# Placement of the down-weight block operations in the first feed-forward block and of the seven-product down projection in the third, in a hybrid decoder layer

## The chip, the core and the metric

The program runs on one core of one Trainium2 chip. The metric is the device time of one execution in microseconds (us). The engines are TensorE (PE, with its weight loads shown as PEld), VectorE (DVE), ScalarE (ACT), GpSimd (POOL) and the DMA queue that SyncE issues (SP). Each engine runs its own instructions in order and waits at an instruction until the semaphores it needs are there.

## The reference

One layer of a decoder is computed in float32 for a prompt of 2048 positions and 32 sample positions: RMSNorm, an input projection, dilated attention beside a spatial gating unit, an output projection with residual, and then the part that this case is about:

```
def _swiglu(x, g, w_gate, w_up, w_down):
    h = _rmsnorm(x, g)
    return (jax.nn.silu(h @ w_gate) * (h @ w_up)) @ w_down
...
    x = x + _swiglu(x, norm2_g, w_gate, w_up, w_down)
```

The model width is 1024 and the hidden width 2816, which is 22 column tiles of 128. A final RMSNorm follows.

## The kernel before

**Precision.** Every matrix product is made of three products of a high and a low part (high with high, high with low, low with high). The high part is a rounded copy made by ACT, the low part is the difference, made by POOL or DVE (`both_halves`: ACT at L1604, then POOL at L1608).

**Blocks and units.** The 16 prompt tiles are worked in three blocks: tiles 0 to 5, 6 to 11, and 12 to 15. The third block also takes the sample rows along. Inside a block the loop runs over f, the 22 column tiles of the hidden width, and for each f over q from 0 to 6: one seven-product (Strassen-like) scheme makes gate and up together from seven products instead of eight. `product` (L1714 to L1716) is one such gate or up product: four steps k of three matmuls, into one of four PSUM banks named ps_m. Behind each product DVE or ACT combine its result (L1726 on ACT for q=0; on DVE L1728, L1730, L1740, L1743 with L1744, L1746 and L1752 for q=1 to 6). An even f and the odd f behind it form a pair; the hidden values of a pair go through the down projection together, while the next even f is worked.

**First block: plain down projection.** `down_unit` projects one tile: two halves of six matmuls each (L1975), each half into one of two PSUM banks named ps_o, and then DVE adds the half to the accumulator (L1977). A half can only start when the add of the half two before it has freed its bank. For even f the loop puts two tiles behind q=3, two behind q=4 and two behind q=5.

**First block: preparing the down weights of the later blocks.** The second and third block use a seven-product scheme for the down projection too, and its operands are made once, in the first block, from the raw weight rows of a pair in the buffers `fe` (rows2[1]) and `fd` (rows2[0]): four differences `block_sum` (DVE, L1653), then for each a rounded high part `block_high` (ACT, L1661), a low part `block_low` (DVE, L1666) and its store to memory `block_keep` (SP, L1670). The table `FIRST_DOWNS` says behind which (f mod 2, q) each is issued, and with a third number, behind which point of the down tiles. `first_downs_ahead` reads it.

**Other first-block work in those queues.** ACT scales fresh weights (L1576, in groups of eight), POOL forms their sums (L1588, L1591, L1594, L1597) and low halves (L1608), and ACT rounds those sums (L1604, `op<-pair` or `op<-fr`).

**Second and third block: seven products.** Class `Seven` queues the down projection of a pair as single products (`one`, L1917, three matmuls of 512 columns, and a DVE add at L1919) and, in the third block, sample products (`sample`, L1925 and L1928). In the third block that is 14 products and 4 sample products for each pair. `begin` fills the queue when the even f reaches a given q, and `woven` returns a step function that `product` calls behind each of its four k: it pops one entry. All entries alternate between two PSUM banks, so each waits for the add of the entry two before it. `even`, `odd_a`, `odd_b` and `odd_c` make the seven left operands from the hidden values (high part on ACT L1834, low part on DVE L1835, sums on DVE L1859, L1869, L1875, L1882), and `plan` says behind which q `even` runs and behind which q the right operands `whole[d]` are loaded (SP, L1830).

**Order.** There is no planner here: within each engine the instructions stand in the order in which the loops write them. `later(n, ...)` puts work off by n `tick`s, one per product or down tile.

Of the kernel before, what the change touches and what calls it, by code (L numbers as in the profile page):

```python
# [28 lines left out]
NF = FF // P  # L29
# [36 lines left out]
def hymba_step(ctx: ExitStack, tc: tile.TileContext, A: dict, O: dict):  # L66
# [6 lines left out]
    left, low, right = ExitStack(), ExitStack(), ExitStack()  # L73
# [585 lines left out]
    for n in range(len(first) + 4):  # L659
        if n >= 4:  # L660
            (w_split if first[n - 4][0] == "w" else x_half_split)(*first[n - 4][1:])
        if n < len(first):
            if first[n][0] == "w":
                k = first[n][1]
# [39 lines left out]
    for half in range(2):  # L704
        for ki, kind in enumerate(ORDER[half]):
            for gi, tiles in enumerate(GROUPS):
                start = ((half * 5 + ki) * 3 + gi) * 8
                for k in range(KD):
                    if start == 0:

                        for j in range(3):
                            n = 3 * k + j
# [7 lines left out]
                for j, tj in enumerate(tiles):  # L720
# [23 lines left out]
                    else:  # L744
                        layer_norm(e + 1, t, lambda t=t: zn["g", t], P)

                        f = e + 4 + (3 if tj in (4, 5) else 0)
                        at(f, "turn", gate_split, t)
                        if tj % 4 == 3:
                            g = t // 4  # L750
# [448 lines left out]
    for h in range(H):  # L1199
# [4 lines left out]
        if end:  # L1204

            x = s0 - NI
            d = stats_of(h, dve, steps_of(x, (11, "misc"), (13, "early"), (14, "early")))
# [8 lines left out]
        if ahead:  # L1216
            d = stats_of(h, pool, steps_of(s0, (2, "misc"), (4, "early"), (5, "early")))
            weights_of(d, steps_of(s0, (5, "misc"), (6, "early"), (6, "misc"), (7, "early"), (7, "misc"), (9, "early"), (9, "mid")))
            chunks = ((11, 14), (11, 16), (14, 19), (18, 22))
        else:  # L1220
            d = stats_of(h, pool, steps_of(s0, (3, "misc"), (5, "early"), (6, "early")))
# [11 lines left out]
    for i, it in enumerate(items):  # L1233
        x, h, n = B0 + i, it["h"], it["n"]
# [443 lines left out]
    def split_down(f):  # L1678
# [1 line left out]
        split_sb(*wd[f % FC], raws.pop(("d", f)))  # L1680

    FIRST_DOWNS = {(1, 2): ((split_down, 0),), (1, 4): ((block_sum, 0), (down_keep, -1), (split_down, 0)), (1, 6): (),
                   (0, 1): ((block_sum, 2), (down_keep, -1)), (0, 2): ((block_sum, 1),),
                   (0, 3): ((block_sum, 3), (block_high, 0), (block_high, 2)), (0, 3, 1): ((block_low, 0), (block_low, 2)),
                   (0, 4): ((block_keep, 0), (block_keep, 2), (block_high, 1)), (0, 4, 1): ((block_low, 1),),
                   (0, 5): ((block_keep, 1), (block_high, 3)), (0, 5, 1): ((block_low, 3),), (0, 6): ((block_keep, 3),)}

    def first_downs_ahead(f, q, *end):

        g = f // 2 if f % 2 else f // 2 - 1  # L1690
        for fn, x in FIRST_DOWNS.get((f % 2, q, *end), ()):
            if fn is split_down:
                split_down(f - (q == 2))
            elif 0 <= g < NF // 2 - 1:
                if fn is block_keep:
                    fn(g, x)
                elif fn is down_keep:
                    fn(f + x)
                else:
                    fn(x)  # L1700
# [82 lines left out]
    class Seven:  # L1783
# [146 lines left out]
        def woven(self, f, q):  # L1930

            if not self.todo:
                return None
            left = {"n": 4 * (7 - q) if f % 2 == 0 and f + 2 == NF else 10 ** 6}

            def step(k):
                n = -(-len(self.todo) // max(left["n"], 1)) if left["n"] < 10 ** 6 else 1
                left["n"] -= left["n"] < 10 ** 6
                for _ in range(min(n, len(self.todo))):
                    fn, *args = self.todo.pop(0)  # L1940
                    fn(*args)
            return step

        def plan(self, f, q):

            g = f // 2
            if f % 2 and g + 1 < NF // 2:
                if q == 1:
                    self.later_places()
                if q in (3, 4):  # L1950
                    self.even(q - 3)
                for d in ((), (0, 1), (2,), (3,), (4,), (5,), (6,))[q]:
                    self.load(g, d)
            elif f % 2 == 0 and f:
                if q == 0 and self.B.last:
                    self.load(g - 1, 7)
                if f + 2 == NF and q == 3:
                    load_down(f)

    def down_unit(B, i, h):  # L1960
        tick()
        nr = P if B.rows[i] == P else 2 * SR
        for half in range(2):
            cs = slice(half * 512, (half + 1) * 512)
            ps = ps_o()
            for z in range(FC):
                dh, dl = wd[z]
                hh, hl, hs_ = h[z]
                if B.rows[i] == P:
                    ts = slice(i * P, (i + 1) * P)  # L1970
                    pairs = ((hh[:, ts], dh), (hh[:, ts], dl), (hl[:, ts], dh))
                else:
                    pairs = ((hs_, dh), (hs_, dl))
                for y, (l_, r_) in enumerate(pairs):
                    pe.matmul(ps[0:nr], l_, r_[:, cs], start=(z == 0 and y == 0),  # L1975
                              stop=(z == FC - 1 and y == len(pairs) - 1))
            dve.tensor_add(B.acc[i][0:nr, cs], B.acc[i][0:nr, cs], ps[0:nr])  # L1977
# [261 lines left out]
    for bi, B in enumerate(blocks):  # L2239
# [17 lines left out]
        def one(u, q):  # L2257
# [8 lines left out]
                    if f + 2 < NF:  # L2266
                        load_source(f + 2, q - 3)
            tick()
            if st and f and f % 2 == 0 and q == 4:
                st.begin(f // 2 - 1)  # L2270
            product(B, u, q, st and st.woven(f, q))
            if st and u["b"] == B.nt:
# [40 lines left out]
                if q == 3:  # L2313
                    split_down(f)

        def downs_of(pair, a, b):
            for i in rows[a:b]:
                down_unit(B, i, pair)

        for n, u in enumerate(units):  # L2320
            u["n"] = n
            for q in range(7):
                one(u, q)
                if not st and u["f"] % 2 == 0 and u["f"] > 0 and 3 <= q < 6:
                    downs_of((B.h[0], B.h[1]), *((0, 2), (2, 4), (4, 9))[q - 3])
                    first_downs_ahead(u["f"], q, 1)
        pair = (B.h[0], B.h[1])
        if B.last:
            first_downs(B, 0, 1, pair)
# [129 lines left out]
```

## Time and profile before

| what | value |
|---|---|
| time, median of 3 runs | 2613.41 us (2610.51 to 2614.55) |
| time of the profiled execution | 2611.25 us |
| span of the profiled execution | 2609.5 us, so 1.75 us lie around it |
| PE / DVE / ACT / POOL busy | 94% / 67% / 47% / 51% of the span |
| granted TensorE clock, mean | 0.985 |
| first feed-forward block, even-odd pairs | about 1060 to 1560 us of the span |
| third block, gate and up products | about 2190 to 2576 us |

The profile is one execution recorded by the hardware profiler. In its timeline a row gives the start, the duration, the engine, the line of the kernel, the operation with output and inputs, and the count; in brackets stands how long the engine had been idle before it and which engine's instruction released it.

### The profile page before, as it was taken

Reading aid. Unit: us, or ns where it says so; the run is one execution under the profiler, and the core shown is the slowest. Engines: PE = TensorE matmul, PEld = TensorE weight load, DVE = VectorE, ACT = ScalarE, POOL = GpSimd, SP = SyncE. Lnnn points to the kernel's source line nnn. Section 1 sums busy time; section 2 is a strip of 40 time slices with the busy share of each in tenths; the row PEclk is TensorE's granted clock in tenths of the full one; section 3 lists DMA queues with packets and bytes.
Section 4 is the critical chain, followed back from the end, with each engine's and each line's share of the span. In section 5 each row is a group of like instructions: output and inputs, shape, how many; then the busy total and the mean of one; then the engine's idle time right before and its main releaser. Section 6 shows DMA issues by size and latency. Waiting matters only on the chain.

```text
span 2609.5 us, 39833 instructions
## 1 busy us (share of the span) xinstructions
PE 2446.0 (94%) x13448; PEld 2148.1 (82%) x13448; DVE 1738.8 (67%) x3255; ACT 1236.0 (47%) x2634; POOL 1341.1 (51%) x1048
## 2 busy tenths in 40 slices
PE   8999799999999889899999999999999999999996
PEld 6777687678988768888988988999999988888885
DVE  3359676346888866555555566777777776777776
ACT  6414334446877746554554545433333345333333
POOL 2035654123576655776776753544444444555552
PEclk9999899999999999999999999999999999999998
DMA  8764844588687673776776775576767663788773
GB/s 251 219 201 154 277 143 128 180 254 262 188 234 228 171 205 127 254 250 234 258 258 231 253 242 182 190 256 223 246 234 240 244 196 119 294 302 296 272 266 141
DMA packets 355785, 580.74 MB, mean 223 GB/s; under 512 B 29553, under 2 KB 182546, under 8 KB 349694
## 3 DMA queue, kind: packets, MB, share of 16 engines
q1 hardware_dynamic: 350108, 569.16, 66.4%
q10 hardware_dynamic: 5474, 9.04, 1.3%
q8 instruction: 108, 1.77, 0.3%
q14 instruction: 95, 0.78, 0.1%
HBM read 440.44 MB, written 207.77 MB: 248 GB/s over the span
## 4 chain that ended last, share of the span: by engine, by line
PE 37%; DVE 9%; POOL 5%; issue 4%; ACT 3%; DMA 2%; SPq 0%; POOLq 0%; DVEq 0%; ACTq 0%
PE ps_o L1917 8%; PE ps_m L1716 7%; PE ps_m L1715 7%; PE ps_m L1714 7%; PE ps_o L1975 4%; POOL op L1608 2%; ACT fr L1576 1%; DVE acc L1919 1%; POOL dw L140 1%; DVE fe L1845 1%; DMA ab_d<-fr 1%; PE ps_o L1925 1%; DVE ao L1835 1%; ACT op L1604 1%; DVE raw L1744 1%
## 5 line engine op out<-in xcount | busy, mean ns | idle before, releaser
L1608 POOL TENSOR_TENSOR op<-fr,op 128x512 fp32r<-128x512 f32 x385 | 523.2, 1369 | 456.2 <-ACT op L1604 431.0
L1716 PE MATMUL ps_m<-xh,op 128*128 128x384 f32 (+5 forms) x1932 | 610.8, 316 | 0.8 <-POOL op L1608 0.8
L1714 PE MATMUL ps_m<-xh,op 128*128 128x384 f32 (+5 forms) x1932 | 609.9, 316 | 1.0 <-DVE zn L1746 1.0
L1715 PE MATMUL ps_m<-xl,op 128*128 128x384 f32 (+5 forms) x1932 | 609.9, 316 | 0.0
L1714 PEld LDWEIGHTS ps_m<-xh,op 128*128 128x128 f32 x1932 | 363.6, 188 | 21.7 <-issue 1.3
L1715 PEld LDWEIGHTS ps_m<-xl,op 128*128 128x128 f32 x1932 | 363.5, 188 | 17.3
L1716 PEld LDWEIGHTS ps_m<-xh,op 128*128 128x128 f32 x1932 | 363.6, 188 | 1.0 <-POOL op L1608 1.0
L1919 DVE TENSOR_TENSOR acc<-acc,ps_o 128x512 f32<-128x512 f32 x350 | 238.2, 685 | 99.9 <-PE ps_o L1917 95.2
L1604 ACT ACTIVATE op<-fr 128x512 fp32r<-128x512 f32 x396 | 240.1, 621 | 105.1 <-POOL op L1608 59.5
L1975 PE MATMUL ps_o<-dw,hw 128*128 128x512 f32 x840 | 206.9, 398 | 29.7 <-DVE acc L1977 29.7
L1763 ACT ACTIVATE ps_t<-zn 128x384 f32<-128x384 f32 (+1 forms) x126 | 58.5, 465 | 353.9 <-DVE zn L1746 217.6
L1975 PEld LDWEIGHTS ps_o<-dw,hw 128*128 128x128 f32 x840 | 156.7, 190 | 71.8 <-DVE acc L1977 40.6
L320 PE MATMUL ps_s<-wh,xh 128*128 128x512 f32 x480 | 197.6, 412 | 7.0 <-ACT xh L137 6.1
L321 PE MATMUL ps_s<-wl,xh 128*128 128x512 f32 x480 | 191.8, 400 | 1.3 <-DVE wl L228 1.3
L322 PE MATMUL ps_s<-wh,xl 128*128 128x512 f32 x480 | 191.1, 398 | 0.0
L1917 PE MATMUL ps_o<-op,ao 128*128 128x512 f32 x450 | 129.7, 398 | 15.9 <-DVE acc L1919 13.5
L1977 DVE TENSOR_TENSOR acc<-acc,ps_o 128x512 f32<-128x512 f32 x142 | 94.8, 683 | 69.6 <-PE ps_o L1975 69.5
L1608 POOL TENSOR_TENSOR op<-pair,op 128x512 fp32r<-128x512 f32 x63 | 81.2, 1295 | 114.0 <-ACT op L1604 111.4
L320 PEld LDWEIGHTS ps_s<-wh,xh 128*128 128x128 f32 x480 | 92.7, 193 | 37.4 <-issue 8.3
L321 PEld LDWEIGHTS ps_s<-wl,xh 128*128 128x128 f32 x480 | 92.9, 194 | 20.0 <-DVE wl L228 2.6
L322 PEld LDWEIGHTS ps_s<-wh,xl 128*128 128x128 f32 x480 | 92.3, 192 | 20.6 <-DVE xl L140 0.3
L1917 PEld LDWEIGHTS ps_o<-op,ao 128*128 128x128 f32 x450 | 79.3, 188 | 28.2 <-DVE acc L1919 20.9
(542 smaller groups left out, 5540.4 us busy)
## 6 DMA issues: line engine op xcount, KB each, us to landing
fr<-ab_d SPq DMA_DIRECT2D x308, 256.0 KB
db<-td_d SPq DMA_DIRECT2D x60, 512.0 KB
out_ks_dram<-in_cache_k_dram SPq DMA_DIRECT2D x56, 512.0 KB
out_vs_dram<-in_cache_v_dram SPq DMA_DIRECT2D x56, 512.0 KB
ab_d<-fr SPq DMA_DIRECT2D x88, 256.0 KB
bd_d<-dw SPq DMA_DIRECT2D x40, 512.0 KB
op<-bd_d SPq DMA_DIRECT2D x40, 512.0 KB
raw<-in_w_in_dram SPq DMA_DIRECT2D x72, 256.0 KB
```

Of the source, the lines that this page charges most:

```text
L320: pe.matmul(o[j], xh[:, k, :], wh, start=(k == 0), stop=False)
L321: pe.matmul(o[j], xh[:, k, :], wl, start=False, stop=False)
L322: pe.matmul(o[j], xl[:, k, :], wh, start=False, stop=(k == KD - 1))
L1604: act.activation(ops[f, j][0], ab[f][j], AF.Copy)
L1608: (pool if f or j in POOL_LOW else dve).tensor_sub(lo_, ab[f][j], hi.bitcast(F32))
L1714: pe.matmul(out, wh[:, ks], xh[:, :, k], start=(k == 0), stop=False)
L1715: pe.matmul(out, wh[:, ks], xl[:, :, k], start=False, stop=False)
L1716: pe.matmul(out, wl[:, ks], xh[:, :, k], start=False, stop=(k == 3))
L1917: pe.matmul(ps, l_, r_, start=(new and x == 0), stop=(x == 2), skip_group_check=True)
L1919: dve.tensor_add(acc, acc, ps)
L1975: pe.matmul(ps[0:nr], l_, r_[:, cs], start=(z == 0 and y == 0), stop=(z == FC - 1 and y == len(pairs) - 1))
L1977: dve.tensor_add(B.acc[i][0:nr, cs], B.acc[i][0:nr, cs], ps[0:nr])
```

## The change

In the first block the four `block_sum` move one product earlier (behind q=0, 1 and 2 instead of 1, 2 and 3), `block_high` 0 and 2 move from behind q=3 to behind q=2, and `first_downs_ahead` is called behind each single down tile, so that one `block_low` stands behind a tile where before one or two stood behind both tiles of a q.

In the third block, except for its last pair, `begin` runs at q=5 instead of q=4, and `woven` pops an entry behind k=0, 1 and 2 but none behind k=3. The 18 entries of a pair then end at q=3 of the odd f instead of q=1. `even` runs behind q=4 and 5 of the odd f instead of 3 and 4, and the eight loads of right operands come behind q=3 to 6 of the odd f and q=0 and 1 of the next even f, in the order 2, 3, 0, 1, 4, 5, 6, 7 instead of 0 to 7. The second block is worked as before.

```
     FIRST_DOWNS = {(1, 2): ..., (1, 4): ..., (1, 6): (),
-                   (0, 1): ((block_sum, 2), (down_keep, -1)), (0, 2): ((block_sum, 1),),
-                   (0, 3): ((block_sum, 3), (block_high, 0), (block_high, 2)), (0, 3, 1): ((block_low, 0), (block_low, 2)),
-                   (0, 4): ((block_keep, 0), (block_keep, 2), (block_high, 1)), (0, 4, 1): ((block_low, 1),),
-                   (0, 5): ((block_keep, 1), (block_high, 3)), (0, 5, 1): ((block_low, 3),), (0, 6): ((block_keep, 3),)}
+                   (0, 0): ((block_sum, 2),), (0, 1): ((block_sum, 1), (down_keep, -1)),
+                   (0, 2): ((block_sum, 3), (block_high, 0), (block_high, 2)), (0, 3, 0): ((block_low, 0),), (0, 3, 1): ((block_low, 2),),
+                   (0, 4): ((block_keep, 0), (block_keep, 2), (block_high, 1)), (0, 4, 0): ((block_low, 1),),
+                   (0, 5): ((block_keep, 1), (block_high, 3)), (0, 5, 0): ((block_low, 3),), (0, 6): ((block_keep, 3),)}
...
-            left = {"n": 4 * (7 - q) if f % 2 == 0 and f + 2 == NF else 10 ** 6}
+            left = {"n": 4 * (7 - q)}
             def step(k):
-                n = -(-len(self.todo) // max(left["n"], 1)) if left["n"] < 10 ** 6 else 1
-                left["n"] -= left["n"] < 10 ** 6
+                n = -(-len(self.todo) // max(left["n"], 1)) if f + 2 == NF else k < 3 or not self.B.last
+                left["n"] -= 1
...
-                if q in (3, 4):
-                    self.even(q - 3)
-                for d in ((), (0, 1), (2,), (3,), (4,), (5,), (6,))[q]:
+                if q - self.B.last in (3, 4):
+                    self.even(q - self.B.last - 3)
+                for d in (((), (), (), (2, 3), (0, 1), (4,), (5,)) if self.B.last else ((), (0, 1), (2,), (3,), (4,), (5,), (6,)))[q]:
                     self.load(g, d)
             elif f % 2 == 0 and f:
-                if q == 0 and self.B.last:
-                    self.load(g - 1, 7)
+                if q < 2 and self.B.last:
+                    self.load(g - 1, (6, 7)[q])
...
-            if st and f and f % 2 == 0 and q == 4:
+            if st and f and f % 2 == 0 and q == (5 if B.last and f + 2 < NF else 4):
                 st.begin(f // 2 - 1)
...
-        def downs_of(pair, a, b):
+        def downs_of(pair, a, b, f, q):
             for i in rows[a:b]:
                 down_unit(B, i, pair)
+                first_downs_ahead(f, q, i - a)
...
-                    downs_of((B.h[0], B.h[1]), *((0, 2), (2, 4), (4, 9))[q - 3])
-                    first_downs_ahead(u["f"], q, 1)
+                    downs_of((B.h[0], B.h[1]), *((0, 2), (2, 4), (4, 9))[q - 3], u["f"], q)
```

Three places show what stands where now. The first is DVE in the first block, at an even f, from its product q=1 to the end of the two down tiles behind q=3. L1653 is a `block_sum`, L1666 a `block_low`, L1977 an add of a half tile. Before:

```order
L1728 TENSOR_TENSOR raw<-zn,ps_m_11553 128x384
L1653 TENSOR_TENSOR fe<-fd,fe 128x512
L1730 TENSOR_TENSOR zn<-zn,ps_m_11578 128x384
L1653 TENSOR_TENSOR fd<-fd,fe 128x512
L1740 TENSOR_TENSOR zn<-raw,ps_m_11603 128x384
L1653 TENSOR_TENSOR fd<-fd 128x512
L1977 TENSOR_TENSOR acc_9931<-acc_9931,ps_o_11635 128x512
L1977 TENSOR_TENSOR acc_9931<-acc_9931,ps_o_11643 128x512
L1977 TENSOR_TENSOR acc_9929<-acc_9929,ps_o_11651 128x512
L1977 TENSOR_TENSOR acc_9929<-acc_9929,ps_o_11659 128x512
L1666 TENSOR_TENSOR fe<-fe,zn 128x512
L1666 TENSOR_TENSOR fe<-fe,raw 128x512
```

And now, at the same place:

```order
L1653 TENSOR_TENSOR fe<-fd,fe 128x512
L1728 TENSOR_TENSOR raw<-zn,ps_m_11554 128x384
L1653 TENSOR_TENSOR fd<-fd,fe 128x512
L1730 TENSOR_TENSOR zn<-zn,ps_m_11579 128x384
L1653 TENSOR_TENSOR fd<-fd 128x512
L1740 TENSOR_TENSOR zn<-raw,ps_m_11608 128x384
L1977 TENSOR_TENSOR acc_9931<-acc_9931,ps_o_11635 128x512
L1977 TENSOR_TENSOR acc_9931<-acc_9931,ps_o_11643 128x512
L1666 TENSOR_TENSOR fe<-fe,zn 128x512
L1977 TENSOR_TENSOR acc_9929<-acc_9929,ps_o_11652 128x512
L1977 TENSOR_TENSOR acc_9929<-acc_9929,ps_o_11660 128x512
L1666 TENSOR_TENSOR fe<-fe,raw 128x512
```

Each of the three sums went ahead of one combining step, and the first `block_low` now stands between the adds of the two tiles.

The second place is ACT in the first block, at the same f, from the combining step of q=2 on. L1661 is a `block_high`, L1604 the rounding of gate and up operands, L1576 the scaling of fresh weights:

```order
-L1763 ACTIVATE ps_t_11592<-zn 128x384
-L1604 ACTIVATE op<-pair 128x512
-L1604 ACTIVATE op<-fr 128x512
-L1576 ACTIVATE fr<-fr,g2c 128x128 x8
+L1763 ACTIVATE ps_t_11593<-zn 128x384
+L1604 ACTIVATE op<-pair 128x512
 L1661 ACTIVATE zn<-fe 128x512
 L1661 ACTIVATE raw<-fe 128x512
 L1604 ACTIVATE op<-fr 128x512
 L1576 ACTIVATE fr<-fr,g2c 128x128 x8
+L1604 ACTIVATE op<-fr 128x512
+L1576 ACTIVATE fr<-fr,g2c 128x128 x8
```

The two `block_high` passed one rounding and one group of eight scalings; they still stand behind the rounding of `pair`.

The third place is DVE in the third block, in an odd f, from the combining step of q=3 to the first hidden product of q=6. L1835 and L1869 are the work of `even`. Before:

```order
L1740 TENSOR_TENSOR zn<-raw,ps_m_23524 128x272
L1835 TENSOR_TENSOR ao<-fe,ao 128x256
L1869 TENSOR_TENSOR zn<-fe 128x256
L1743 TENSOR_TENSOR raw<-raw,ps_m_23550 128x272
L1744 TENSOR_TENSOR raw<-raw,ps_m_23524 128x272
L1835 TENSOR_TENSOR ao<-zn,ao 128x256
L1746 TENSOR_TENSOR zn<-zn,ps_m_23574 128x272
L1845 TENSOR_TENSOR zn<-ps_t_23588,raw 128x2x64 x2
```

And now:

```order
L1740 TENSOR_TENSOR zn<-raw,ps_m_23512 128x272
L1743 TENSOR_TENSOR raw<-raw,ps_m_23544 128x272
L1744 TENSOR_TENSOR raw<-raw,ps_m_23512 128x272
L1835 TENSOR_TENSOR ao<-fe,ao 128x256
L1869 TENSOR_TENSOR zn<-fe 128x256
L1746 TENSOR_TENSOR zn<-zn,ps_m_23571 128x272
L1835 TENSOR_TENSOR ao<-zn,ao 128x256
L1845 TENSOR_TENSOR zn<-ps_t_23585,raw 128x2x64 x2
```

`even` moved behind the combining steps of q=4. In the even f that follows, the combining steps of q=4 (L1743, L1744) now stand ahead of the first add of the pair (L1919) instead of behind four of them.

## The prediction

> **What bounds the kernel now.** I read the page, then PE's busy time in stretches, then PE's waits in the two stretches that the change touches, then the timeline of one pair in each.
>
> ```profile
> span 2609.5 us, 39833 instructions
> ...
> 1200.00:1300.00 100.00, 95.53 (x499) 88.14 (x498) 55.01 (x87) 52.83 (x127) 71.56 (x51) 1.00 0.75 253
> 1800.00:1900.00 100.00, 99.89 (x530) 93.49 (x529) 77.44 (x123) 34.05 (x67) 49.52 (x36) 1.00 0.74 247
> 2300.00:2400.00 100.00, 93.16 (x610) 85.19 (x611) 75.81 (x157) 35.38 (x83) 52.68 (x41) 1.00 0.74 274
> ```
>
> Behind the window's length stand PE, PEld, DVE, ACT and POOL busy, then PE's granted clock, the DMA share and GB/s. PE is the bound. The second block (middle row) keeps it busy 99.89%, the first 95.53% and the third 93.16%, all at clock 1.00. What the change can win is those idle shares. PE's waits, in the first block's pairs and in the third block:
>
> ```profile
> PE ps_o L1975 <- DVE acc L1977: 23.5, 17, 5.6
> ...
> PE ps_o L1917 <- DVE acc L1919: 13.5, 9, 1.6
> PE ps_o L1925 <- DVE acc L1919: 8.9, 9, 1.0
> ```
>
> All of it is one kind: a down product waits until DVE has added the result that fills its PSUM bank. That is 23.5 and 22.4 us.
>
> **First block.** One pair in the timeline (start, duration, engine, line; in brackets the idle time ahead):
>
> ```profile
> 1165.11 2.92 PE L1975 MATMUL ps_o<-dw,hw 128*128 128x512 f32 x12
> 1167.65 0.39 PE L1975 MATMUL ps_o<-dw,hw 128*128 128x512 f32 x1
> 1169.23 3.02 PE L1975 MATMUL ps_o<-dw,hw 128*128 128x512 f32 x12 [1.19 <-DVE acc L1977]
> 1174.19 2.92 PE L1975 MATMUL ps_o<-dw,hw 128*128 128x512 f32 x12
> 1178.16 2.14 PE L1975 MATMUL ps_o<-dw,hw 128*128 128x512 f32 x8 [1.05 <-DVE acc L1977]
> ...
> 1164.48 0.68 DVE L1653 TENSOR_TENSOR fe<-fd,fe 128x512 f32<-128x512 f32 x1
> 1165.55 1.32 DVE L1653 TENSOR_TENSOR fd<-fd,fe 128x512 f32<-128x512 f32 x1
> 1167.26 1.31 DVE L1653 TENSOR_TENSOR fd<-fd 128x512 f32<-128x512 f32 x1
> 1168.50 1.27 DVE L1977 TENSOR_TENSOR acc<-acc,ps_o 128x512 f32<-128x512 f32 x2
> 1175.16 0.69 DVE L1666 TENSOR_TENSOR fe<-fe,zn 128x512 fp32r<-128x512 f32 x1 [2.19 <-ACT zn L1661]
> 1176.37 0.55 DVE L1743 TENSOR_TENSOR raw<-raw,ps_m 128x384 f32<-128x384 f32 x1
> 1177.43 1.28 DVE L1977 TENSOR_TENSOR acc<-acc,ps_o 128x512 f32<-128x512 f32 x2
> ...
> 1171.11 0.63 ACT L1604 ACTIVATE op<-pair 128x512 fp32r<-128x512 f32 x1 [4.95 <-POOL pair L1594]
> 1174.51 0.62 ACT L1661 ACTIVATE zn<-fe 128x512 fp32r<-128x512 f32 x1
> ...
> 1168.10 1.61 POOL L1591 TENSOR_TENSOR fr<-fr 128x512 f32<-128x512 f32 x1
> 1169.79 1.29 POOL L1594 TENSOR_TENSOR pair<-fr 128x512 f32<-128x512 f32 x1
> 1171.04 1.29 POOL L1608 TENSOR_TENSOR op<-fr,op 128x512 fp32r<-128x512 f32 x1
> 1172.29 1.29 POOL L1608 TENSOR_TENSOR op<-pair,op 128x512 fp32r<-128x512 f32 x1
> ```
>
> A tile's twelve matmuls start (1167.65 - 1165.11)/11 = 0.23 us apart, so a tile takes 2.77. Tile 1 could start at 1167.88 and starts at 1169.23; tile 3 could start at 1176.96 and starts at 1178.16. Those are the two waits.
>
> *Sums.* DVE's chain to the first add holds the sum at 1167.26. Now the first sum runs before L1728, where DVE sat waiting for ACT, so the second and third sum take the places of the first and second, and the first add follows the combining step at 1167.26 instead of 1168.50. Tile 1 then starts 0.67 + 0.05 behind that, at 1167.98: 1.25 saved. The displaced sum goes behind L1326 into DVE's idle time of 2.86 (at most 1.3 long); its cost is nothing, and if ACT were faster it would be 0.68 to 1.31.
>
> *High parts.* ACT's two L1661 pass one rounding and eight scalings. They stay behind the rounding that waits for POOL's L1594. POOL's L1591 took 1.61 instead of 1.29 beside the third sum, which is gone from there, so L1594 should end about 0.3 earlier: the first L1661 runs at about 1171.25 and ends at 1171.9, against 1174.51. The roundings that come later by 1.2 us feed products four places ahead, each about 2.2 us (1174.19 - 1169.23 - 2.77), so some 8 us of cover; PE has no wait for an operand in these pairs, so it holds; without it each product would wait up to 1.2.
>
> *Low parts.* This is the added wait. DVE now stops at L1666 behind tile 0's adds, until ACT is done at 1171.9; queued behind it are tile 1's adds, and PE's tiles 2 and 3 wait for those. From 1171.9: L1666, two adds (0.6 each), L1666, L1743 and L1744 (1177.43 - 1176.37 = 1.06), an add of 0.7, then tile 3. L1666 has two inputs in SBUF, and such a step took 0.68 where POOL was idle and 1.31 where POOL was running. If both low parts find the port free, tile 3 starts at 1171.9 + 0.65 + 1.25 + 0.65 + 1.06 + 0.7 = 1176.2; if both wait for a POOL step, at 1177.4. Before it was 1178.16, so 0.8 to 2.0 are saved per pair. POOL's rows from 1169.79 to 1173.6 have no gap, which speaks for waiting at the first L1666, while the second falls near POOL's idle time: I take 1.4.
>
> The Trainium skill (SBUF — State Buffer, section "Who interferes with whom") says that a DVE instruction with two SBUF inputs and a GpSimd instruction exclude each other for a whole instruction, whoever comes first going first. The pair 0.68 and 1.31 agrees; strictly by that rule every low part that meets POOL waits, the saving would be the lower 0.8, and the first block would give 7 us instead of 12.5.
>
> Tiles 3 to 5: the third and fourth low parts stand in front of adds that are needed only after q=5 and q=6, 2 us later; nothing. The stores move with the low parts on SP, earlier. Eight pairs have both waits: 8 x 1.4 = 11.2 (ends 6.6 and 16). The first pair has one:
>
> ```profile
> 1071.63 3.78 PE L1975 MATMUL ps_o<-dw,hw 128*128 128x512 f32 x8 [5.63 <-DVE acc L1977]
> ```
>
> There the same chain bounds tile 1, 1.25 earlier, but the low parts may take that back at tiles 2 and 3; with the last pair I count 1.3 (0 to 3). First block: -12.5, ends -6.6 and -19.
>
> **Third block.** One pair:
>
> ```profile
> 2336.59 0.96 PE L1917 MATMUL ps_o<-op,ao 128*128 128x512 f32 x3 [1.49 <-DVE acc L1919]
> 2350.68 0.68 PE L1925 MATMUL ps_o<-op,hs 128*64 128x512 f32 x2 [0.99 <-DVE acc L1919]
> ...
> 2335.51 0.42 DVE L1740 TENSOR_TENSOR zn<-raw,ps_m 128x272 f32<-128x272 f32 x1
> 2335.86 1.47 DVE L1919 TENSOR_TENSOR acc<-acc,ps_o 128x512 f32<-128x512 f32 x2
> 2339.26 0.43 DVE L1743 TENSOR_TENSOR raw<-raw,ps_m 128x272 f32<-128x272 f32 x1
> 2340.09 1.39 DVE L1919 TENSOR_TENSOR acc<-acc,ps_o 128x512 f32<-128x512 f32 x2
> 2356.19 0.44 DVE L1730 TENSOR_TENSOR zn<-zn,ps_m 128x272 f32<-128x272 f32 x1 [1.01 <-PE ps_m L1716]
> 2357.69 0.44 DVE L1740 TENSOR_TENSOR zn<-raw,ps_m 128x272 f32<-128x272 f32 x1 [1.06 <-PE ps_m L1716]
> 2358.05 1.22 DVE L1835 TENSOR_TENSOR ao<-fe,ao 128x256 fp32r<-128x256 f32 x1
> 2359.19 1.51 DVE L1869 TENSOR_TENSOR zn<-fe 128x256 f32<-128x256 f32 x1
> 2362.66 0.49 DVE L1845 TENSOR_TENSOR zn<-ps_t,raw 128x128 f32<-128x128 f32 x2 [0.47 <-ACT ps_t L1763]
> ```
>
> DVE comes late to the pair: its first add starts at 2335.86, the third product is ready at 2336.59 - 1.49 = 2335.10. A product lasts 1.50 (L1730 and L1740 both waited for PE).
>
> *Later start.* The third product is ready one product later, at 2336.60; but L1743 and L1744 (2340.09 - 2339.26 = 0.83) now go ahead of the first add, which ends at 2337.37. The wait would be 0.82 + s, where s is what DVE's queue loses in the odd f ahead. The bank that q=5 writes is freed by the late L1728, so part of this wait may show at L1714.
>
> *Moved `even`.* DVE idles from 2358.0 until q=4's result at 2359.19, does L1743 and L1744 until 2360.0, then L1835 and L1869, 0.35 each unblocked, 1.14 and 1.43 if blocked as in the rows; L1746, ACT's L1763 (0.5), a third L1835. L1845 then comes between 2361.6 and 2364 against 2362.66: s from -1.0 to +1.4. I take +0.5, one step blocked and one in part. So this wait goes from 1.49 to 1.32.
>
> *Three per product.* The wait of 0.99 comes since DVE works on the hidden values of q=6 between two adds. One more k step (1.50/4 = 0.38) now lies between those entries on PE: 0.61.
>
> Per pair -0.17 - 0.38 = -0.55, nine pairs -5; the last pair starts at q=4 behind the later `even`: +0.5. Third block: -4.5; ends 9 x -1.87 = -17 (first wait gone) and 9 x 0.35 + 1.4 = +4.5.
>
> *Loads.*
>
> ```profile
> fr<-ab_d SPq DMA_DIRECT2D x308, 256.0 KB
> db<-td_d SPq DMA_DIRECT2D x60, 512.0 KB
> ...
> 2356.00:2360.00 4.00, 4.00 (x34) 4.00 (x33) 2.75 (x4) 1.78 (x4) 3.02 (x3) 1.00 0.98 353
> ```
>
> The operands of the first product are issued behind q=4 of the odd f, at about 2359, with two others, two `fr` and one 512 KB copy ahead: 2.6 MB, at 353 GB/s 7.4 us from 2357.6, landing at 2365. They are needed eight products after 2357.7, near 2370. The 5 us cover them; beyond that each us late costs 9.
>
> **Rivals.**
> 1. *More is won.* Low parts meet a free port and s is -1: -19 - 17 = -36, so 2575, and from there up to 2585. For it: POOL idles 28% in this stretch. Against: its rows are closed where the low part lands.
> 2. *The gain turns into new waits.* Both low parts are blocked in each pair (-6.6) and s is +1.4 (+4.5): -2, so 2609, with a spread of 2604 to 2613. For it: two of three `even` steps were blocked before.
> 3. *Slower.* L1661 does not get ahead: if the rounding of `pair` comes late and L1661 starts past 1172 with both low parts blocked, or past 1173.2 with both free, the low part that now stands before tile 1's adds costs more than the sums save. At the old 1174.51 the two adds put between the low parts make tile 3 later by 1.3 with the port free, by 2.5 with both blocked: 8 x 1.3 = +10 to 8 x 2.5 = +20, so 2621 to 2631, and from 2613 on for starts between. Against: nothing ahead of it in ACT's queue but the POOL chain, which only loses a contender.
>
> **How the numbers follow.** -12.5 - 4.5 = -17. The profiled execution took 2611.25, so 2594; it lay 2.2 below the median of 2613.41, so the forecast is 2595. Chances: forecast (2585 to 2604) 0.60, more is won 0.13, new waits 0.17, slower 0.10. The measurement tells 0.2%, 5.2 us, from no change. New waits split at 2608: 0.08 of them are faster, 0.09 within; of the slower case 0.02 are within. Faster: 0.60 + 0.13 + 0.08 = 0.81; same 0.11; slower 0.08. The range 2578 to 2610 leaves out the slower case (0.10), the upper part of the new waits (0.05) and the far end of the first rival (0.03).
>
> **What would show it.** First block: the wait ahead of tile 1 below 0.3, L1661 near 6 us behind tile 0's start instead of 9.4, a DVE wait at L1666 for ACT of 1 to 3 us, waits at tiles 2 and 3 that sum to less than 1.2. Third block: waits of about 1.3 and 0.6 per pair and none on a DMA. It is wrong if the pairs of f keep their length, if L1661 hasn't moved, or if PE waits for POOL or a load.

## The result, and the profile after

The changed kernel takes 2606.99 us (median of 20 runs, 2600.48 to 2613.77); the kernel before took 2612.16 us beside it (median of 20 runs). The ratio is 0.9977, with a 95% interval of 0.9969 to 0.9985. That is 5.2 us less, where 2595 us and 17 us less were forecast. The time lies inside the stated range (2578 to 2610), but the gain is less than a third of the forecast; it lies where the second rival, a gain that turns into new waits, had put it.

The page and PE's busy time in the same three stretches, of the changed kernel:

```profile
span 2604.8 us, 39882 instructions
```

```profile
1200.00:1300.00 100.00, 97.32 (x509) 89.74 (x508) 61.06 (x90) 52.58 (x128) 75.05 (x52) 1.00 0.73 250
1800.00:1900.00 100.00, 99.89 (x525) 92.91 (x524) 76.84 (x121) 32.46 (x63) 49.70 (x36) 1.00 0.71 242
2300.00:2400.00 100.00, 94.59 (x623) 86.41 (x621) 74.65 (x159) 36.18 (x87) 52.75 (x42) 1.00 0.78 274
```

The second block is untouched. PE is busier in both other blocks, by 1.8 and 1.4 points. PE's waits (total, times, longest), in the first block from 1060 to 1560 us and in the third block:

```profile
PE ps_o L1975 <- DVE acc L1977: 19.4, 14, 4.3
...
PE ps_o L1917 <- DVE acc L1919: 12.6, 19, 2.5
PE ps_m L1714 <- DVE raw L1728: 7.9, 9, 1.1
```

The 23.5 us that the prediction shows for the first block are from 1060 to 1500 us. Over the stretch used here the kernel before has more:

```profile
PE ps_o L1975 <- DVE acc L1977: 26.8, 21, 5.6
```

So 26.8 became 19.4 us, in 14 pieces instead of 21. In the third block 22.4 became 20.5, in 28 pieces instead of 18. But the 20.5 hold the last pair's wait of 2.48, and the 22.4 leave out the last pair's 1.85, which the view puts down to a load. Without the last pair 22.4 became 18.0. Now the first block's pair, in the timeline of the changed kernel (tile 0 starts at 1164.75):

```profile
1164.75 5.91 PE L1975 MATMUL ps_o<-dw,hw 128*128 128x512 f32 x24
1174.10 4.27 PE L1975 MATMUL ps_o<-dw,hw 128*128 128x512 f32 x17 [1.33 <-DVE acc L1977]
...
1165.19 1.32 DVE L1653 TENSOR_TENSOR fd<-fd 128x512 f32<-128x512 f32 x1
1166.89 1.50 DVE L1977 TENSOR_TENSOR acc<-acc,ps_o 128x512 f32<-128x512 f32 x2
1171.62 1.83 DVE L1666 TENSOR_TENSOR fe<-fe,zn 128x512 fp32r<-128x512 f32 x1 [3.23 <-ACT zn L1661]
1173.37 1.27 DVE L1977 TENSOR_TENSOR acc<-acc,ps_o 128x512 f32<-128x512 f32 x2
1174.57 0.68 DVE L1666 TENSOR_TENSOR fe<-fe,raw 128x512 fp32r<-128x512 f32 x1
...
1170.97 0.61 ACT L1661 ACTIVATE zn<-fe 128x512 fp32r<-128x512 f32 x1
...
1170.36 1.30 POOL L1608 TENSOR_TENSOR op<-fr,op 128x512 fp32r<-128x512 f32 x1
1171.61 1.29 POOL L1608 TENSOR_TENSOR op<-pair,op 128x512 fp32r<-128x512 f32 x1
```

Tiles 0 and 1 run as one piece of 24 matmuls: the wait ahead of tile 1 is gone. The two waits of before, 1.19 and 1.05, became one of 1.33 ahead of tile 2. The reason stands in the DVE and POOL rows: the first high part is ready at 1171.58, DVE begins its low part at 1171.62, and POOL had begun a step at 1171.61. The low part lasts 1.83 us, POOL's 1.29 and then 0.54 more, and tile 1's adds queue behind it. All nine first low parts from the second pair on take 1.83, with POOL's start at most 0.01 ahead: both sides start from the same event, the end of POOL's L1594 (1170.40 here), and ACT's rounding and first high part take about as long as POOL's step at 1170.36. From pair to pair the sum at 1165.19 recurs at 1212.83: 47.64 us, against 48.48 before.

The third block, in the changed kernel, one pair, and the wait at the last pair (f = 20):

```profile
2364.47 0.36 PE L1714 MATMUL ps_m<-xh,op 128*128 128x272 f32 x1 [0.85 <-DVE raw L1728]
2367.75 0.96 PE L1917 MATMUL ps_o<-op,ao 128*128 128x512 f32 x3 [0.51 <-DVE acc L1919]
2375.80 0.96 PE L1917 MATMUL ps_o<-op,ao 128*128 128x512 f32 x3 [0.61 <-DVE acc L1919]
...
2544.41 1.31 PE L1917 MATMUL ps_o<-op,ao 128*128 128x512 f32 x3 [2.48 <-DVE acc L1919]
...
2351.75 0.42 DVE L1740 TENSOR_TENSOR zn<-raw,ps_m 128x272 f32<-128x272 f32 x1
2353.87 1.49 DVE L1835 TENSOR_TENSOR ao<-fe,ao 128x256 fp32r<-128x256 f32 x1
2355.29 0.42 DVE L1869 TENSOR_TENSOR zn<-fe 128x256 f32<-128x256 f32 x1
2356.85 0.43 DVE L1835 TENSOR_TENSOR ao<-zn,ao 128x256 fp32r<-128x256 f32 x1 [0.80 <-ACT ao L1834]
2357.20 0.48 DVE L1845 TENSOR_TENSOR zn<-ps_t,raw 128x128 f32<-128x128 f32 x2
```

The second wait is 0.61, as forecast. The first comes in two pieces, 0.85 at L1714 and 0.51 at L1917, 1.36 together; 1.32 was forecast. Yet a pair (2364.47 to the same row at 2400.00) lasts 35.53, only 0.14 less than the 35.66 of before. And behind the 2.48 us wait the granted clock (third number from the end) is low, in the windows of the changed kernel:

```profile
2544.00:2546.00 2.00, 1.59 (x5) 1.21 (x6) 1.29 (x3) 0.91 (x2) 1.53 (x2) 0.71 0.75 299
2546.00:2548.00 2.00, 2.00 (x8) 1.72 (x7) 1.12 (x2) 0.00 (x0) 0.98 (x1) 0.50 1.21 497
2548.00:2550.00 2.00, 2.00 (x11) 1.72 (x10) 1.26 (x2) 0.15 (x1) 0.00 (x0) 0.93 0.05 21
```

Before, the last pair's wait was 1.85 us and the clock stayed at 1.00 behind it.

### The profile page after: what moved, and what is told of

Its sections match the earlier page's. It is cut to its first block, busy times and chain, and to the rows that moved or that the text cites. A ratio compares the mean times of both kernels' runs of the same rounds, so it can differ in the third digit from the quotient of the medians.

```text
span 2604.8 us, 39882 instructions
## 1 busy us (share of the span) xinstructions
PE 2457.2 (94%) x13448; PEld 2155.3 (83%) x13448; DVE 1748.9 (67%) x3255; ACT 1235.8 (47%) x2634; POOL 1346.4 (52%) x1048
## 4 chain that ended last, share of the span: by engine, by line
PE 40%; DVE 7%; POOL 5%; issue 4%; DMA 2%; ACT 2%; SPq 0%; POOLq 0%; DVEq 0%; ACTq 0%
PE ps_m L1716 8%; PE ps_m L1715 8%; PE ps_m L1714 8%; PE ps_o L1917 8%; PE ps_o L1975 5%; POOL op L1608 2%; DVE acc L1919 1%; POOL dw L140 1%; DMA ab_d<-fr 1%; DVE fe L1845 1%; POOL pair L1588 1%; PE ps_o L1925 1%; PE ps_o L1414 1%; PE ps_o L1416 1%; PE ps_o L1415 1%
## 5 line engine op out<-in xcount | busy, mean ns | idle before, releaser
L1714 PE MATMUL ps_m<-xh,op 128*128 128x384 f32 (+5 forms) x1932 | 611.2, 316 | 8.9 <-DVE raw L1728 7.9
L1714 PEld LDWEIGHTS ps_m<-xh,op 128*128 128x128 f32 x1932 | 363.7, 188 | 31.5 <-ACT pair L1834 9.6
L1919 DVE TENSOR_TENSOR acc<-acc,ps_o 128x512 f32<-128x512 f32 x350 | 238.5, 686 | 115.5 <-PE ps_o L1917 111.6
L1604 ACT ACTIVATE op<-fr 128x512 fp32r<-128x512 f32 x396 | 239.3, 621 | 124.0 <-issue 74.3
L1917 PE MATMUL ps_o<-op,ao 128*128 128x512 f32 x450 | 131.0, 401 | 13.1 <-DVE acc L1919 12.6
L1977 DVE TENSOR_TENSOR acc<-acc,ps_o 128x512 f32<-128x512 f32 x142 | 95.2, 682 | 27.0 <-PE ps_o L1975 25.2
L613 POOL TENSOR_TENSOR vl<-kv,vh 100x512 fp32r<-100x512 f32 (+1 forms) x32 | 46.1, 1441 | 109.7 <-ACT vh L607 35.5
```

The costliest lines, as they stand in the source:

```text
L1604: act.activation(ops[f, j][0], ab[f][j], AF.Copy)
L1714: pe.matmul(out, wh[:, ks], xh[:, :, k], start=(k == 0), stop=False)
L1917: pe.matmul(ps, l_, r_, start=(new and x == 0), stop=(x == 2), skip_group_check=True)
L1919: dve.tensor_add(acc, acc, ps)
```

## The experiments

Each kernel is the changed kernel with the edits shown, timed beside the kernel before. A pair's length is the distance of one row from the same row of the next pair.

| kernel | us, median | ratio to before (95%) | first block pair | third block pair |
|---|---|---|---|---|
| before | 2612 to 2614 | 1 | 48.48 | 35.66 |
| changed | 2606.99 | 0.9977 (0.9969 to 0.9985) | 47.64 | 35.53 |
| first block's part alone | 2603.22 | 0.9969 (0.9958 to 0.9980) | 47.63 | 35.66 |
| third block's part alone | 2610.38 | 1.0001 (0.9991 to 1.0011) | 48.48 | 35.53 |
| low parts behind both tiles | 2605.73 | 0.9973 (0.9964 to 0.9982) | 47.55 | 35.53 |
| sums alone in the first block | 2614.50 | 1.0001 (0.9989 to 1.0013) | 48.18 | 35.53 |
| high parts back | 2631.95 | 1.0067 (1.0050 to 1.0083) | 50.87 | 35.53 |
| low parts a tile later | 2585.86 | 0.9899 (0.9886 to 0.9912) | 45.89 | 35.53 |
| high parts one product earlier | 2590.80 | 0.9906 (0.9890 to 0.9922) | 45.93 | 35.53 |
| `even` back | 2590.41 | 0.9918 (0.9905 to 0.9930) | 47.63 | 33.87 |
| `even` back, start at q=4 | 2603.38 | 0.9967 (0.9954 to 0.9980) | 47.63 | 35.56 |
| `even` back for the last pair | 2602.35 | 0.9957 (0.9945 to 0.9969) | 47.63 | 35.53 |
| low parts later and `even` back | 2574.22 | 0.9849 (0.9832 to 0.9867) | 45.95 | 33.87 |

**Each part alone.** The edit takes the other part back to the old lines. Expected of the first block's part:

> Only the first block's part of the change. Theory A (what the two traces suggest: the first block won about 6.5 us, 0.84 in each pair, and the third block won nothing): 6.5 below the kernel before, pairs of 47.64 us. Theory B (the first block won the forecast 12.5 and the third block gave 7 back): 12 below, pairs of about 47.1. Theory C (the two blocks share the 5 us evenly): 2.5 below, pairs of about 48.2.

And of the third block's part:

> Only the third block's part. Theory A: between 1 below and 2 above the kernel before; pairs of 35.5 us against 35.7 before, a last wait of about 2.5 us with the clock down behind it. Theory B: 6 to 8 above. The forecast on record: 4.5 below, pairs of 35.1.

The first block's part carries all of the gain, the third block's nothing that can be measured: its pairs win 0.13 or 0.14 each, somewhat over 1 us together, and its last pair loses about 1.8 in the profiled execution.

**Low parts behind both tiles again.** It undoes the added stop of DVE in front of tile 1's adds.

```
-(0, 3, 0): ((block_low, 0),), (0, 3, 1): ((block_low, 2),)
+(0, 3, 1): ((block_low, 0), (block_low, 2))
-(0, 4, 0): ((block_low, 1),)
+(0, 4, 1): ((block_low, 1),)
-(0, 5, 0): ((block_low, 3),)
+(0, 5, 1): ((block_low, 3),)
```

> The change with both low parts of a q put back behind both of its down tiles; sums and high parts stay early. Theory A (the chain through both low parts, L1743, L1744 and an add sets tile 3, wherever the first low part stands): the wait of 1.3 ahead of tile 2 goes, one of 0.5 to 1.2 ahead of tile 3 comes; 0 to 5 below the changed kernel. Theory B (the low part ahead of tile 1's adds is the whole loss): the wait goes and none comes, 10 below the changed kernel.

From its timeline:

```profile
1130.45 3.01 PE L1975 MATMUL ps_o<-dw,hw 128*128 128x512 f32 x12 [1.31 <-DVE acc L1977]
...
1125.20 1.84 DVE L1666 TENSOR_TENSOR fe<-fe,zn 128x512 fp32r<-128x512 f32 x1 [0.20 <-ACT zn L1661]
1126.97 1.78 DVE L1666 TENSOR_TENSOR fe<-fe,raw 128x512 fp32r<-128x512 f32 x1
```

The wait is as long and stands ahead of tile 3 instead of tile 2. So one down weight operation behind each tile costs or wins nothing that these times can tell: two low parts, L1743 and L1744 still run one behind the other between the high part and an add that PE needs.

**The sums alone.** High and low parts stand as before, only the four sums are early.

```
-(0, 2): ((block_sum, 3), (block_high, 0), (block_high, 2)), (0, 3, 0): ...
+(0, 2): ((block_sum, 3),), (0, 3): ((block_high, 0), (block_high, 2)), (0, 3, 1): ((block_low, 0), (block_low, 2)), ...
```

> The changed kernel with only the sums moved in the first block: `block_high` 0 and 2 and all low parts stand as before. Theory A: the wait ahead of tile 1 goes, and the chain from L1661 (unmoved against ACT and POOL) through two low parts, L1743 and L1744 then sets tile 3 alone: its wait grows from 1.05 by nearly the 1.2 that tile 1 gained, pairs of 48.2 to 48.5 against 48.48 before, and the time 5 to 7 us over the changed kernel, near 2613. Rival: the sums alone carry the gain; pairs near 47.6 as in the changed kernel and 2607 us.

From its timeline:

```profile
1179.50 3.01 PE L1975 MATMUL ps_o<-dw,hw 128*128 128x512 f32 x12 [1.99 <-DVE acc L1977]
...
1176.50 0.69 DVE L1666 TENSOR_TENSOR fe<-fe,zn 128x512 fp32r<-128x512 f32 x1 [3.13 <-ACT zn L1661]
1177.11 0.69 DVE L1666 TENSOR_TENSOR fe<-fe,raw 128x512 fp32r<-128x512 f32 x1
```

The gain at tile 1 reappears as a longer wait at tile 3. Here both low parts find the port free, 0.69 each; in the kernel above, three microseconds earlier against ACT and POOL, they took 1.84 and 1.78. The earlier high parts come 2.9 us sooner behind the sums (1124.56 - 1118.78 against 1175.86 - 1167.19), and 2.2 of that go back to POOL in the two low parts; the rest is the difference between 1.99 and 1.31.

One of its pairs lasts 49.77 instead of 48.2. The wait there is the same, but the clock fell behind it (the wait of the pair before, and this one; then a window behind each):

```profile
1324.00 3.01 PE L1975 MATMUL ps_o<-dw,hw 128*128 128x512 f32 x12 [1.97 <-DVE acc L1977]
1372.17 4.33 PE L1975 MATMUL ps_o<-dw,hw 128*128 128x512 f32 x12 [1.97 <-DVE acc L1977]
...
1325.00:1327.00 2.00, 2.00 (x10) 1.64 (x9) 0.69 (x1) 0.00 (x0) 0.00 (x0) 1.00 0.53 197
1374.00:1376.00 2.00, 2.00 (x6) 1.54 (x6) 0.67 (x1) 0.00 (x0) 0.00 (x0) 0.50 0.31 116
```

**The high parts back.** This is the prediction's third rival built: the low part stands ahead of tile 1's adds and the high part comes at the old time.

```
-(0, 2): ((block_sum, 3), (block_high, 0), (block_high, 2)),
+(0, 2): ((block_sum, 3),), (0, 3): ((block_high, 0), (block_high, 2)),
```

> The changed kernel with `block_high` 0 and 2 back behind q=3, behind one more rounding and eight scalings on ACT, and the rest of the change as it is. It tests the prediction's third rival. Theory A: the first low part, now ahead of tile 1's adds, waits for L1661 at the old time, about 9.4 us behind tile 0's start instead of 6.2; the wait ahead of tile 2 grows from 1.33 by 2.5 to 3, PE's clock may fall behind it as it does behind the first pair's 4.3 us: 23 to 35 us over the changed kernel, 2630 to 2642. Rival: DVE's idle time absorbs it, under 10 us.

From its timeline:

```profile
1180.74 0.69 DVE L1666 TENSOR_TENSOR fe<-fe,zn 128x512 fp32r<-128x512 f32 x1 [6.13 <-ACT zn L1661]
...
1182.08 7.34 PE L1975 MATMUL ps_o<-dw,hw 128*128 128x512 f32 x24 [3.09 <-DVE acc L1977]
```

It is slower than before by 0.67%, as that rival said it would be from such a start (2631.95 us; the rival had 2621 to 2631). Of the 3.23 us by which its pair exceeds the changed kernel's, 1.76 are the longer wait; behind it 24 matmuls take 7.34 us, where two tiles without a wait take 5.64 to 5.94, at a granted clock of 0.76 in the five microseconds from 1180. In one pair of the eight the clock stayed at 1.00 behind a wait of 3.07, and that pair lasts 49.82; the others last 50.75 to 50.89.

**Low parts one tile later.** It takes one of the two low parts out of the chain.

```
-(0, 3, 0): ((block_low, 0),), (0, 3, 1): ((block_low, 2),),
-(0, 4): ((block_keep, 0), (block_keep, 2), (block_high, 1)), (0, 4, 0): ((block_low, 1),),
-(0, 5): ((block_keep, 1), (block_high, 3)), ...
+(0, 3, 1): ((block_low, 0),),
+(0, 4): ((block_keep, 0), (block_high, 1)), (0, 4, 0): ((block_low, 2),), (0, 4, 1): ((block_low, 1),),
+(0, 5): ((block_keep, 2), (block_keep, 1), (block_high, 3)), ...
```

> The changed kernel with the low parts one tile later each: 0 behind tile 1, 2 behind tile 2, 1 behind tile 3, 3 behind tile 4, and the stores of 2 and 1 behind q=5. Theory A: what is left of the wait is the chain of two low parts, L1743 and L1744 ahead of tile 2's adds; with one low part (up to 1.8 us) taken out of it, the waits of 1.33 ahead of tile 2 and 3 are gone: pairs of 46.3 instead of 47.64, about 11 us under the changed kernel. Rival: the low parts meet POOL's steps wherever they stand and hold the adds of tiles 3 and 4 instead; pairs of 47.3 to 47.7, 0 to 3 us.

From its timeline:

```profile
1171.06 5.67 PE L1975 MATMUL ps_o<-dw,hw 128*128 128x512 f32 x24
...
1170.08 1.83 DVE L1666 TENSOR_TENSOR fe<-fe,zn 128x512 fp32r<-128x512 f32 x1 [0.23 <-ACT zn L1661]
1174.63 1.25 DVE L1666 TENSOR_TENSOR fe<-fe,raw 128x512 fp32r<-128x512 f32 x1
```

Tiles 2 and 3 now run as one piece too. Both low parts are blocked by POOL (1.83 and 1.25), and nobody waits for that. The pair is 1.75 shorter than the changed kernel's, more than the 1.33 that the bracket shows, and the profiled span falls from 2604.8 to 2587.6, by 17.2: eight pairs at 1.75 make 14.0, and the rest comes from the loop's last pair, which in the changed kernel waits 1.36 and 0.97 and here not at all. The median falls by 21, which is uncertain by about 4.

**High parts one product earlier.** The same aim by another way: DVE's idle 3.23 us ahead of the first low part are filled.

```
-(0, 1): ((block_sum, 1), (down_keep, -1)),
-(0, 2): ((block_sum, 3), (block_high, 0), (block_high, 2)), ...
+(0, 1): ((block_sum, 1), (block_high, 0), (block_high, 2), (down_keep, -1)),
+(0, 2): ((block_sum, 3),), ...
```

> The changed kernel with `block_high` 0 and 2 behind q=1 instead of q=2, so ahead of the ACT rounding that waits for POOL's L1594. Theory A: in the changed kernel DVE is idle for 3.23 us behind tile 0's adds, waiting for the first high part; with it there, the first low part runs in that gap and the second behind tile 1's adds without the first: the wait ahead of tile 2 is gone, pairs of 46.3, about 11 us under the changed kernel. Rival: ACT's two extra steps of 0.62 hold the combining steps of q=2 and the transposes; the gain is under 5 us, with a wait on ps_m or ps_t shown.

The first low part runs at 1164.61 in its timeline, directly behind tile 0's adds, and PE shows 24 matmuls in 5.94 and in 5.64 us with no wait. The pair is 45.93, the time like that of the kernel above. The two were both meant to break the chain from L1661 to tile 2 or 3, and both do.

**`even` back.** Only this step of the third block is undone.

```
-                if q - self.B.last in (3, 4):
-                    self.even(q - self.B.last - 3)
+                if q in (3, 4):
+                    self.even(q - 3)
```

> The change with the work of even put back behind q=3 and 4 of the odd f in the third block; later start, three per product and load places stay. Theory A (moving even costs VectorE about 0.9 us in each pair and undoes what the later start wins): the two parts of the first wait fall from 0.85 and 0.5 to a sum of about 0.8 or less, the last pair's wait falls from 2.5 to 1.9 and the clock stays up there: 6 to 10 below the changed kernel, pairs of 34.8 to 35.1. Theory B (VectorE is late for another reason, such as its steps beside POOL in the even f): no pair shorter by more than 0.2, at most 2 below.

From its timeline:

```profile
2362.57 0.96 PE L1917 MATMUL ps_o<-op,ao 128*128 128x512 f32 x3
...
2348.24 0.42 DVE L1740 TENSOR_TENSOR zn<-raw,ps_m 128x272 f32<-128x272 f32 x1
2348.59 0.41 DVE L1835 TENSOR_TENSOR ao<-fe,ao 128x256 fp32r<-128x256 f32 x1
2348.93 0.41 DVE L1869 TENSOR_TENSOR zn<-fe 128x256 f32<-128x256 f32 x1
2351.97 0.49 DVE L1845 TENSOR_TENSOR zn<-ps_t,raw 128x128 f32<-128x128 f32 x2 [0.47 <-ACT ps_t L1763]
...
2348.78 3.15 POOL L1608 TENSOR_TENSOR op<-fr,op 128x512 fp32r<-128x512 f32 x2 [0.88 <-DMA db<-td_d]
```

The first wait has vanished, and more was won than I had expected: 16.6 us against the changed kernel. From L1740 to L1845 DVE needs 3.73 us here, 5.45 in the changed kernel and 4.97 before. In the kernel before, POOL had begun a step at 2357.69 and DVE came to L1835 at 2358.05: the two steps of `even` took 1.22 and 1.51. Here DVE comes 0.19 ahead of POOL, both steps take 0.41, and POOL's two steps take 3.15 instead of 2.72.

**`even` back, start at q=4.** It stands on top of the edit above and leaves the spacing by threes alone.

```
-            if st and f and f % 2 == 0 and q == (5 if B.last and f + 2 < NF else 4):
+            if st and f and f % 2 == 0 and q == 4:
```

> `even` back behind q=3 and 4 as in the 2590 us kernel, and the products begin at q=4 again, still three per gate or up product. It leaves only the spacing of the third block's change. Theory A: the later start is what took the first wait away; with the start at q=4 the wait of about 1.49 ahead of the third product is back, the second stays at 0.61: pairs of 35.3, against 33.86 with the later start and 35.66 before, and about 2603 us. Rival: the spacing by threes is what gained; pairs stay near 33.9 and the time near 2590.

From its timeline:

```profile
2471.26 0.96 PE L1917 MATMUL ps_o<-op,ao 128*128 128x512 f32 x3 [1.69 <-DVE acc L1919]
2482.90 0.96 PE L1917 MATMUL ps_o<-db,ao 128*128 128x512 f32 x3 [0.61 <-DVE acc L1919]
```

The first wait is back, and `even` is blocked as before (1.31 and 1.50 at 2456.97 and 2458.20). The spacing wins its 0.38 on the second wait, loses 0.20 on the first, and a pair gains 0.10. The later start is what wins, when `even` stays.

**`even` back for the last pair only.**

```
+                z = self.B.last and f + 3 < NF
-                if q - self.B.last in (3, 4):
-                    self.even(q - self.B.last - 3)
+                if q - z in (3, 4):
+                    self.even(q - z - 3)
```

> The changed kernel, but in the last odd f (f = 21 has no pair behind it; the step concerns the pair whose products run at f = 20) `even` stays behind q=3 and 4. Theory A: the 2.48 us wait ahead of f = 20's first products comes from the moved `even`, and the half granted clock behind it (windows 2546:2550 of the changed kernel) from that wait. Then the wait falls to about 0.8, as with `even` moved back everywhere, the clock stays near 1.00, steady pairs stay at 35.53, and the time is about 3 us under the changed kernel (1.65 of wait, about 1.5 of slow matmuls). Rival: the clock falls there for another reason; then only about 1.6 us go and the low clock stays.

From its timeline, and the windows behind that wait:

```profile
2541.31 0.97 PE L1917 MATMUL ps_o<-op,ao 128*128 128x512 f32 x3 [0.83 <-DVE acc L1919]
```

```profile
2541.00:2543.00 2.00, 1.69 (x7) 1.24 (x8) 1.63 (x3) 0.82 (x2) 1.63 (x2) 1.00 1.13 448
2543.00:2545.00 2.00, 2.00 (x13) 1.67 (x12) 1.49 (x4) 0.00 (x0) 0.91 (x1) 1.00 1.02 407
```

The wait is 1.65 shorter and the clock stays at 1.00. The span is 4.3 us shorter; 1.5 of them were there ahead of the third block, where the code is the same, so 2.8 belong to the last pair: 1.65 of wait and about 1.2 of slow matmuls. The kernel with the low parts behind both tiles separates the two: it has the changed kernel's third block and a wait of 2.49 there, but the clock stayed at 1.00 behind it, and from the L1740 of f = 19 to that of f = 21 it needs 35.72 us where the changed kernel needs 37.17.

**Both corrections together.** The edits of low parts a tile later and of `even` back.

> The low parts one tile later each (the 2586 us kernel) and `even` back behind q=3 and 4 (the 2590 us kernel), together in the changed kernel. Theory A: the two waits stand in different stages and add up: pairs of 45.9 in the first block and 33.9 in the third, about 2586 - 16.6 = 2569 us. Rival: the end of the third block, or a stage between, takes some of it back: 2575 to 2585.

2574.22 us, 5 above the sum of the two but with a span of 2571.0 against 2587.6 for the first correction alone, 16.6 less. This is the fastest kernel of the study, 1.5% under the kernel before. Its waits in the same two stretches:

```profile
PE ps_o L1975 <- DVE acc L1977: 6.3, 4, 4.3
...
PE ps_o L1917 <- DVE acc L1919: 6.8, 11, 0.8
```

## Why the prediction was wrong

It named the right waits and the right port, and mis-sized four terms of its sum. Of the 17 - 5.2 = 11.8 us that are missing, the traces place 11: the pairs of the first block lack 8 x 0.56 = 4.5, its first and last pair 1.5, the pairs of the third block 9 x 0.41 = 3.7 and its last pair 1.3. That the time falls into the second rival's spread is in part luck: only the first of the two low parts was blocked and s was 0.48, where that rival has both blocked and an s of 1.4.

| step | forecast | measured |
|---|---|---|
| *Sums* | wait ahead of tile 1 gone | gone |
| *High parts* | L1661 about 6 us behind tile 0's start instead of 9.4 | 6.2 |
| *Low parts* | first blocked 1.31, second free 0.65 | 1.83 and 0.68 |
| first block, per pair | -1.4 | -0.84 |
| first block, first and last pair | -1.3 | +0.2 |
| *Later start* and *Moved even*, first wait | 1.32 | 0.85 + 0.51 = 1.36 |
| *Moved even*, s | +0.5 | 5.45 - 4.97 = +0.48 |
| *Three per product* | 0.99 to 0.61 | 0.61 |
| third block, per pair | -0.55 | -0.14 |
| third block, last pair | +0.5 | about +1.8 |
| *Loads* | covered | no wait of PE on a load |

*Low parts* is the first step that failed. I took 1.31 as the price of a blocked step, from sums that had met a POOL step already under way. A step that comes just behind POOL's start waits for all of it: 1.29 and 0.54 of its own. That is 0.52 more than the price, and the pair gained 0.56 less than forecast. With 1.83 for the first low part and 0.65 for the second, the prediction's chain puts tile 3 at 1177.39, 12.28 behind tile 0, a saving of 0.8; in the changed kernel the add that frees tile 3's bank ends 12.15 behind tile 0. The chain was right, and what showed as a wait was its first link, the low part ahead of tile 2. The rule that the prediction named, in the Trainium skill (SBUF — State Buffer, section "Who interferes with whom"), agrees with these rows: whoever came first held the port for the whole instruction, POOL at 1171.61, DVE at 2348.59 in the kernel with `even` back. Its reading there, with both low parts blocked, gave the right saving of 0.8 for another reason, since the second low part was free; and with 1.31 for both, the prediction's own sum gives 1177.5 and a saving of 0.6, not 1177.4 and 0.8.

*First and last pair.* The first pair's wait fell from 5.63 to 4.32, as the sums had it, but the stretch from the block's first product (1058.82 before, 1060.03 after) to tile 0 of the second pair (1116.64 and 1117.13) only by 0.72: the matmuls behind that wait run at half clock in both kernels, for 4.3 us before and for 5.6 in the changed one. In the loop's last pair the waits were 1.19 and 0.44 and are 1.36 and 0.97, and the stretch from its tile 0 to the block's last tile grew by 0.94. Whole first block: 501.68 to 495.22 us, 6.5 won where 12.5 were forecast.

*Third block.* Each wait came out as forecast, and the pair did not. The step that failed is to count a wait at its bracket. Two starts of matmuls without a wait are 0.12 to 0.13 apart; at 2364.47 the start before is 2363.34, so 1.01 are lost there and 0.08 at the next step, 1.09 where the bracket says 0.85. At 2367.75 it is 0.77 for 0.51; in the kernel before, at 2336.59, 1.76 for 1.49. Each interruption costs about 0.25 beyond its bracket. The change turned two interruptions into three, which takes 0.25 off the 0.51 of brackets that it saved. Another 0.1 per pair stays open; it is lost in the kernel with the spacing alone too. Counted in the same way, the first block's pair loses 2.78 at its two waits before. Now it loses 1.61 at the one wait, and 0.22 at tile 1 and 0.12 at tile 3, where no bracket stands: 1.95, less by 0.83, which is the pair's gain.

*Last pair.* The wait grew by 0.63, close to the +0.5, and in the profiled execution the clock fell to half behind it for 3.4 us (from the three windows above); those 1.2 us or more were not in the sum.

The weighing of `even` was right for the change as it is, and wrong in what it passed over: its formula, a first wait of 0.82 + s, says that the later start alone decides if s is below -0.8. With `even` left where it was, s is 3.73 - 4.97 = -1.24, and the wait is gone, as the run shows. I had priced only the move. Why DVE arrives ahead of POOL there, and not in the kernel that starts at q=4, was not tested. The rows only show that POOL's step at 2348.78 came behind an ACT rounding (L1604, 2348.07) that had itself waited for POOL's step before, while in the other kernel ACT began that rounding at 2456.01 without such a wait, and POOL its step at 2456.70, 0.27 ahead of DVE.

## What to carry to other kernels

When a chain of small steps stands between a producer and an add that PE waits for, moving its links about only moves the wait; count what remains in the chain behind its last input, and take a link out or start the chain where the engine idles. For a VectorE step with two SBUF inputs, price a block at what is left of the neighbouring GpSimd step, at worst all of it, plus its own time, and ask which of the two comes first, since a shift of some tenths of a microsecond decides it. A wait's bracket is a lower bound of what it costs: here removing a wait of 1.33 us won 1.75, and splitting one wait into two lost about half of what the sum of brackets seemed to win. Count the distance from start to start instead.

## What the runs showed of the hardware

A VectorE step with two SBUF inputs that meets a GpSimd step under way lasts the rest of that step and about 0.55 us more. The low parts of these kernels, 0.68 or 0.69 us when free, show it: 1.83 where POOL's step of 1.29 had begun 0.01 earlier, 1.44 at 0.40, 1.27 at 0.57 and 1.11 at 0.72. So a price read from one row, such as 1.31, is the price of one offset.

The granted clock can fall behind short waits in the middle of a busy stretch. Behind a PE wait of 1.85 us (before) or 2.04 (`even` back, start at q=4) it stayed at 1.00. At the last pair seven kernels of this study have a wait of 2.48 to 2.50: in six the clock fell to between 0.50 and 0.56 in one of the next windows of 2 us and was back within about 6 us; in the seventh, with the low parts behind both tiles, it stayed at 1.00 behind 2.49. In the first block of the kernel with the sums alone it fell behind one wait of eight of 1.94 to 1.99, and with the high parts back it stayed at 1.00 behind one of eight of 3.03 to 3.09. So the length alone does not decide between 1.97 and 3.07 us. Where the clock falls it costs 1.0 to 1.6 us beside the wait: a pair of 49.77 against 48.17, of 50.85 against 49.82, of 37.17 against 35.72. The Trainium skill (TensorE: Matmul & The Clock Gate, "Part 1: The HAM clock gate") speaks of a half rate after an idle window of about 3.4 us that runs freely, whatever the kernel does. That a like wait has both outcomes agrees with a free-running window; that a wait which the profile gives as 1.97 or 2.48 is enough differs from the figure there, and the measurement decides.
